# Encoder layer on one core: low parts of the first layer a step later, a norm in two steps, banks of attention's drain laid out anew

## The chip, the cores and the metric

The kernel runs on one core of a Trainium2 chip. The metric is the time of one execution on the device in microseconds (us); less is better. The core's engines work side by side, each through its own instructions in order: TensorE (PE in the profile, its weight loads PEld), VectorE (DVE), ScalarE (ACT), GpSimd (POOL), and SyncE (SP), which issues the DMAs. They wait for each other through semaphores. TensorE writes its results to PSUM, which has 8 banks; one bank holds 128 x 512 values of 32 bits.

## The reference

One encoder layer over 2048 tokens of width 1024, in 32-bit floating point. Cut to what matters here:

```
h = rms_norm(x);  z = h @ W_in
y_a = mlstm_group(...)                 # 4 heads, forward and backward
y_b = mla_group(...)                   # 4 heads, softmax over all keys
x = x + concat(y_a, y_b) @ w_out       # output projection, residual
h = rms_norm(x, g_ffn_norm)
x = x + square(relu(h @ w_ff1)) @ w_ff2   # 1024 -> 4096 -> 1024
```

## The kernel before

**Split products.** Every operand of a large matmul is split into a high part (a rounded copy, `fp32r`, made by ScalarE) and a low part (source less high part, a subtraction that VectorE makes, or POOL where `eng` says so): `split`, L44 to L52. `mm3` then issues three matmuls, high by high (L63), and two of a high and a low part (L64 and L65). In the trace a line of `split` is seen for all its callers, so one goes by the tiles' names.

**Stages.** The input projection takes the first 467 us, attention until some 1182 us, with the mLSTM's steps between its blocks; then come the output projection (`OutProj`), the feed-forward's first layer from 1372 us to about 2032 us, and the second layer.

**Attention.** A pair of a head and 256 queries is a block; there are 32. For each, `score` fills a bank `ps`, VectorE scales it into `p` and takes the maximum (L1016, L1020), ScalarE takes the exponential (L1027), `transpose_group` transposes into a bank `ptp` and splits that into `pth` and `ptl`, `pv` adds up in one bank `pv` for the block, and `out` scales that bank into `y` (L1063). `split_v` makes `vh` and `vl` of the values. There are 3 banks for `ps` and one for `pv`. While the last blocks drain, the weights of the output projection are split (`woh`, `wol`) and the first token tile is prepared: its mLSTM half is transposed into a bank (`pm`), split, and stored in ring buffers `r`.

**Output projection.** For each of 16 token tiles `prep_y` transposes into the bank `ypt` (pool `psY`) and splits into ring buffers; `project` issues the matmuls into two of the four banks of `psO` (`po`); `residual` adds the result to x (L1285). The last two tiles are projected together, with their residuals last. In the same time the operands of the first layer are prepared: tiles `h0` to `h6`, each of four pieces loaded into staging buffers `raw` and split into `h0h`, `h0l` and so on (`pieces_on`, `h_split`). The pools of PSUM take their banks in the order in which they are opened.

**First layer.** It is computed in blocks by the Strassen-Winograd scheme, with 7 products in place of 8. `layer1` runs over n = 0 to 31 (16 column blocks of W1 for each of two halves of the tokens); each n has 7 products of 12 matmuls into a bank `pu` (6 banks, `psF`), the evacuations (`evacuate`, L1500 and ScalarE's relu and square L1503, L1504), and combinations of results (`u_combine`, L1537). The order of the work is written by hand as generators that are advanced between the products: `wsteps` (`weights1`) makes the high and low parts of W1 in ring buffers `r`, some products ahead (`ahead`), and the sums of W1's blocks (`sw`, and in place in `w1raw`, L1377); `extra` is, one after the other, the remaining pieces of the first half's operands, `tokens` (norm, transposes `dpt`, combinations and stores of the second half's tokens) and `exchange` (the second half's operands are loaded into the low tiles and split in place while the first half's products finish, in n = 14 to 16, L1434 and L1435). The norm (`normalise`) sums squares on ScalarE, takes the root on POOL (`nr`, L59) and scales on VectorE (L1309).

Of the kernel before, what the change touches and what calls it, by code (L numbers as in the profile page):

```python
# [8 lines left out]
F32 = mybir.dt.float32  # L9
# [4 lines left out]
ALU = mybir.AluOpType  # L14
AX = mybir.AxisListType
PSUM = bass.MemoryType.PSUM
DRAM = bass.MemoryType.DRAM

P = 128
# [20 lines left out]

class Ctx:
    pass


def split(nc, hi, lo, src, g=None, eng=None):

    if g is None:
        nc.scalar.copy(hi, src)  # L48
        (eng or nc.vector).tensor_tensor(lo, src, hi.bitcast(F32), op=ALU.subtract)  # L49
    else:  # L50
        nc.scalar.activation(hi, src, AF.Copy, scale=g)
        nc.vector.scalar_tensor_tensor(lo, src, g, hi.bitcast(F32), op0=ALU.mult, op1=ALU.subtract)  # L52
# [872 lines left out]
def attention(c, keep, drain, project):  # L925

    nc, tc = c.nc, c.tc
    with ExitStack() as st:
# [46 lines left out]
        def split_v(h, j):  # L975
            raw = vraw.pop((h, j))
            vh = vp.tile([P, 4, DV], F32R, name="vh")
            vl = vp.tile([P, 4, DV], F32R, name="vl")
            split(nc, vh, vl, raw, eng=nc.gpsimd)
            V[h, j] = vh, vl  # L980

        def load_q(h, j):
# [67 lines left out]
        def pv(b, j):  # L1050
            h = b // NB
            if j == 0:
                pvs[b] = psV.tile([P, 256], F32, name="pv")
            th, tl = pts.pop((b, j))
            vh, vl = V[h, j]
            for k in range(4):
                mm3(nc, pvs[b], vh[:, k, :], vl[:, k, :], th[:, k, :], tl[:, k, :],
                    j == 0 and k == 0, j == 3 and k == 3)
# [25 lines left out]
        N = NH * NB  # L1084
# [93 lines left out]
class OutProj:  # L1178
# [48 lines left out]
    def open(self, ent):  # L1227
        pool = self.c.tc.tile_pool
        self.sp = ent(pool(name="o_s", bufs=2, reuse_waits="tile"))
        self.psT = ent(pool(name="o_psT", bufs=2, space=PSUM, reuse_waits="tile"))  # L1230
        self.psY = ent(pool(name="o_psY", bufs=1, space=PSUM, reuse_waits="tile"))
        self.psO = ent(pool(name="o_ps", bufs=4, space=PSUM, reuse_waits="tile"))

    def load_y(self, s):
        c, nc = self.c, self.c.nc
# [52 lines left out]
    def normalise(self, s):  # L1288
        x1 = self.x.pop(s)
        xs = [self.c.e[:, j, :] for j in range(2)]  # L1290
        normalise(self.c, self.sp, [x1[:, 0:512], x1[:, 512:]], xs, xs)

    def transposed(self, s):
        q = s % 2
# [4 lines left out]
def normalise(c, sp, x, out, junk):  # L1299

    nc = c.nc
    ms = sp.tile([P, 2], F32, name="nms")
    r = sp.tile([P, 1], F32, name="nr")
    for j in range(2):
        nc.scalar.activation(junk[j], x[j], AF.Square, scale=D ** -0.5, accum_out=ms[:, j:j + 1])
    nc.gpsimd.tensor_tensor(ms[:, 0:1], ms[:, 0:1], ms[:, 1:2], op=ALU.add)
    rsqrt(c, r, ms[:, 0:1], 1)
    for j in range(2):
        nc.vector.tensor_scalar(out[j], x[j], r, None, op0=ALU.mult)  # L1309

# [26 lines left out]
class FeedForward:  # L1337
# [41 lines left out]
    def w1_split(self, n, op):  # L1379
        if n < self.NU - 3:  # L1380
            w = self.ring.tile([P, 2, 4, P], F32R)
        else:
            w = self.ring.pool.tile([P, 2, 4, P], F32R, name="r0")
        wh, wl = w[:, 0], w[:, 1]
        split(self.c.nc, wh, wl, self.w1_part(n, WOPS[op]))
        self.w1[n, op] = wh, wl

    def weights1(self):

        N = 2 * self.NU  # L1390
        self.nsplit = 0
        self.w1_combine(0, "S1")
        self.w1_combine(0, "S2")
        for n in range(N):
            for q in range(7):
                self.w1_split(n, q)
                self.nsplit += 1
                yield
                if q == 0:
                    self.w1_combine(n, "S3")  # L1400
                elif q == 2:
                    self.w1_combine(n, "S4")
                elif q == 5 and n + 1 < N:
                    self.w1_combine(n + 1, "S1")
                elif q == 6:
                    if n + 2 < N:
                        self.load_w1(n + 2)
                    if n + 1 < N:
                        self.w1_combine(n + 1, "S2")
                yield  # L1410

    def h_load(self, g, op, k):
        nc = self.c.nc
# [13 lines left out]
    def exchange(self):  # L1427


        c, nc = self.c, self.c.nc  # L1430
        todo = []

        def place(hi, lo):
            nc.scalar.copy(hi, lo.bitcast(F32))  # L1434
            nc.vector.tensor_tensor(lo, lo.bitcast(F32), hi.bitcast(F32), op=ALU.subtract)  # L1435

        def load(hi, lo, src):
            nc.sync.dma_start(lo.bitcast(F32), src)
            todo.append((hi, lo))

        first = [[self.stage.tile([P, 512], F32R, name="raw") for _ in range(4)] for _ in range(2)]
        second = [[self.ring.pool.tile([P, 2, 512], F32R, name="r1") for _ in range(2)] for _ in range(2)]
        for k in range(4):
            load(first[0][k], first[1][k], c.d_h[1, 0, :, k, :])
            if k % 2:
                yield
        for k in range(2):
            load(second[0][k], second[1][k], c.d_h[1, 1, :, 2 * k:2 * k + 2, :])
        yield
        for _ in range(4):  # L1450
            place(*todo.pop(0))
            yield
        nxt = [first, [[t[:, k, :] for t in s for k in range(2)] for s in second]]
        for p in range(12):
            if p < 5:
                pool = self.hp if p < 3 else self.hp1
                hi, lo = (pool.tile([P, 4, 512], F32R, name=f"h{p}{part}") for part in "hl")
                nxt.append([[t[:, k, :] for k in range(4)] for t in (hi, lo)])
                for k in range(0, 4, 2):
                    load(hi[:, k:k + 2, :], lo[:, k:k + 2, :], c.d_h[1, p + 2, :, k:k + 2, :])  # L1460
            if p < 7:
                self.H[p] = nxt[p]
            place(*todo.pop(0))
            yield

    def h_pieces(self, g, todo):
# [78 lines left out]
    def tokens(self):  # L1545

        c, nc = self.c, self.c.nc
        for i in range(4):
            b = []
            for q in range(2):  # L1550
                t = 8 + 4 * q + i
                for j in range(2):
                    x = self.stage.tile([P, 512], F32, name="raw")
                    nc.sync.dma_start(x, c.d_x1[t * P:(t + 1) * P, j * 512:(j + 1) * 512])
                    b.append(x)
            junk = self.stage.tile([P, 512], F32, name="raw")
            for _ in range(4):
                yield
            for q in range(2):
                x = b[2 * q:2 * q + 2]  # L1560
                normalise(c, self.sp, x, x, [junk, junk])
                for _ in range(4):
                    yield
                transpose_x(c, self.psT, x, x)
                yield
            tt = [self.stage.tile([P, 512], F32, name="raw") for _ in range(3)]
            tt.append(junk)
            yield from combine_x(c, b, tt)
            store_x(c, 1, i, b, tt)
            for _ in range(4):  # L1570
                yield

    def layer1(self, extra):
        N = 2 * self.NU
        prev = None
        for n in range(N):
            g, f = divmod(n, self.NU)
            if n == 1:
                extra = self.tokens()
            elif n == self.NU - 2:  # L1580
                for _ in extra:
                    pass
                extra = self.exchange()
            for p in range(7):
                self.product(n, p)
                ahead = 7 * n + p + 1 + (5 if 0 < n < self.NU - 3 else 3)
                todo = min(2, ahead - self.nsplit)
                for i in range(todo):
                    next(self.wsteps, None)
                    if i + 1 < todo:  # L1590
                        next(self.wsteps, None)
                self.flush()
                if prev:
                    self.evacuate(*prev)
                prev = n, p, self.ps
                if todo > 0:
                    next(self.wsteps, None)
                if n > 0 and 1 <= p <= 4:
                    self.u_combine(n - 1, f"S{p}")
                next(extra, None)  # L1600
                if n == 0:
                    next(extra, None)
                if n == N - 1 and p == 2:
                    self.first2()
        return prev
# [145 lines left out]
def out_and_ffn(c):  # L1751
    tc = c.tc
    with ExitStack() as s_stage:
        with ExitStack() as s_e:
# [10 lines left out]
            with ExitStack() as s_y:  # L1765
# [45 lines left out]
                po = o.project(NT - 2, NT - 1)  # L1811
                s_wo.close()
                ff.open_h1(s_h1.enter_context)
                next(ff.wsteps)
                next(ff.wsteps)
                for _ in range(3):
                    pieces_on(4)
                for i in range(2):
# [53 lines left out]
```

## Time and profile before

| | us |
|---|---|
| median of 3 runs | 2649.92 (2648.83 to 2651.17) |
| the profiled execution | 2649.61 |
| its span | 2647.7 |
| TensorE busy | 2587.3 |
| VectorE busy | 1660.6 |
| ScalarE busy | 1201.9 |
| mean granted clock of TensorE | 0.995 |

The span runs from the first to the last instruction of the profiled execution; the execution's own time is 1.9 us longer. Busy is the time in which an engine had an instruction at work. The granted clock is the share of its full 2.4 GHz that TensorE was given; it knows two levels, 0.5 (1.2 GHz) and 1.

### The profile page before, as it was taken

To read this page: it belongs to the slowest core of one execution; us is meant where nothing else is said; L and a number is where in the kernel's file an instruction comes from. 1 tells how busy PE (TensorE), PEld (TensorE's weight loads), DVE (VectorE), ACT (ScalarE), POOL (GpSimd) and SP (SyncE) were. 2 spreads that over 40 slices of the span, in tenths; PEclk is the share of its full clock that TensorE was granted. 3 is DMA by queue.
4 is the path that set the end of the run, shared out by engine and by line. 5 is a ranking of instruction groups with operands and counts; after the bars stand their busy time and mean duration, and the time that the engine had idled before them with its cause. 6 is when DMAs were issued, how large, how long until landed. Compare 5 with 4: busy or idle time off the path is not lost. (4 is left out here: it accounts for less than half of the span.)

```text
span 2647.7 us, 37081 instructions
## 1 busy us (share of the span) xinstructions
PE 2587.3 (98%) x13227; PEld 2176.5 (82%) x13227; DVE 1660.6 (63%) x3202; ACT 1201.9 (45%) x2457; POOL 404.8 (15%) x442
## 2 busy tenths in 40 slices
PE   8999999999999999989999999999999999999999
PEld 6888888778888888878888877678887888888887
DVE  5585476655666666654367777777676477676443
ACT  6455443546666666651144444554544333332332
POOL 1211120123224232220000000000000133332000
PEclk9999999999999999999999999999999999999999
DMA  4345244355455464445665555834445744444552
GB/s 152 119 131 162 90 134 137 71 120 131 93 101 123 92 115 98 70 134 176 201 232 169 167 174 166 274 131 164 142 149 203 280 146 148 146 145 143 207 179 99
DMA packets 298293, 391.57 MB, mean 148 GB/s; under 512 B 33217, under 2 KB 187132, under 8 KB 298108
## 3 DMA queue, kind: packets, MB, share of 16 engines
q1 hardware_dynamic: 295804, 385.01, 49.1%
q10 hardware_dynamic: 2304, 4.20, 0.4%
q8 instruction: 104, 1.70, 0.3%
q14 instruction: 81, 0.66, 0.1%
HBM read 256.94 MB, written 132.17 MB: 147 GB/s over the span
## 5 line engine op out<-in xcount | busy, mean ns | idle before, releaser
L63 PE MATMUL pd<-w2h,uh 128*128 128x512 f32 x896 | 348.9, 389 | 1.3 <-ACT w2h L48 0.9
L64 PE MATMUL pd<-w2l,uh 128*128 128x512 f32 x896 | 348.8, 389 | 0.4 <-DVE w2l L49 0.4
L65 PE MATMUL pd<-w2h,ul 128*128 128x512 f32 x896 | 348.7, 389 | 0.0
L49 DVE TENSOR_TENSOR ptl<-ptp,pth 128x512 fp32r<-128x512 f32 x256 | 176.5, 690 | 212.2 <-ACT pth L48 208.3
L49 DVE TENSOR_TENSOR ul<-ur,uh 128x1024 fp32r<-128x1024 f32 x110 | 144.3, 1312 | 247.9 <-ACT uh L48 247.6
L48 ACT CAST uh<-ur 128x1024 fp32r<-128x1024 f32 x110 | 115.5, 1050 | 395.4 <-PE pd L64 382.4
L48 ACT CAST pth<-ptp 128x512 fp32r<-128x512 f32 x256 | 148.9, 584 | 239.0 <-PE ptp L1046 232.3
L1503 ACT ACTIVATE e<-e 128x512 f32<-128x512 f32 x128 | 80.9, 632 | 278.5 <-DVE e L1500 278.5
L63 PEld LDWEIGHTS pd<-w2h,uh 128*128 128x128 f32 x896 | 168.3, 188 | 36.8 <-ACT w2h L48 1.4
L1016 DVE TENSOR_SCALAR_CACHE_REDUCE p<-ps 128x512 f32<-128x512 f32 x256 | 175.0, 684 | 36.1 <-PE ps L1015 35.5
L64 PEld LDWEIGHTS pd<-w2l,uh 128*128 128x128 f32 x896 | 168.3, 188 | 35.5 <-DVE w2l L49 0.7
L65 PEld LDWEIGHTS pd<-w2h,ul 128*128 128x128 f32 x896 | 168.3, 188 | 34.8
L1646 POOL TENSOR_TENSOR r<-wr,r 128x512 f32<-128x512 f32 x48 | 88.5, 1843 | 634.2 <-DMA wr<-in_w 605.9
L49 DVE TENSOR_TENSOR r<-w1raw,r 128x512 fp32r<-128x512 f32 x160 | 110.5, 690 | 103.7 <-ACT r L48 102.5
L1046 PE MATMUL ptp<-ident,p 128*128 128x128 f32 x1024 | 154.3, 274 | 1.3 <-ACT p L1027 0.9
L63 PE MATMUL pz<-wh,hh 128*128 128x512 f32 (+1 forms) x384 | 150.7, 394 | 3.3 <-ACT hh L48 3.3
L1500 DVE TENSOR_TENSOR e<-pu,e 128x512 f32<-128x512 f32 x224 | 150.7, 685 | 3.2 <-PE pu L65 3.2
L65 PE MATMUL pz<-wh,hl 128*128 128x512 f32 (+1 forms) x384 | 151.0, 393 | 0.0
L64 PE MATMUL pz<-wl,hh 128*128 128x512 f32 (+1 forms) x384 | 150.8, 393 | 0.0
L63 PE MATMUL pv<-pth,vh 128*128 128x256 f32 x512 | 145.8, 285 | 4.3 <-DVE y L1063 2.5
L64 PE MATMUL pv<-ptl,vh 128*128 128x256 f32 x512 | 145.8, 285 | 1.2 <-DVE ptl L49 1.0
L65 PE MATMUL pv<-pth,vl 128*128 128x256 f32 x512 | 145.3, 284 | 0.0
(395 smaller groups left out, 6584.1 us busy)
## 6 DMA issues: line engine op xcount, KB each, us to landing
d_u<-e SPq DMA_DIRECT2D x224, 256.0 KB
ur<-d_u SPq DMA_DIRECT2D x110, 512.0 KB
w1raw<-in_w SPq DMA_DIRECT2D x64, 512.0 KB
wr<-in_w SPq DMA_DIRECT2D x96, 256.0 KB
raw<-in_w_in SPq DMA_DIRECT2D x48, 256.0 KB
xt<-in_x SPq DMA_DIRECT2D x16, 512.0 KB
mb<-d_M SPq DMA_DIRECT2D x32, 256.0 KB
r<-in_x SPq DMA_DIRECT2D x16, 512.0 KB
```

Source lines behind the costliest of these rows:

```text
L48: nc.scalar.copy(hi, src)
L49: (eng or nc.vector).tensor_tensor(lo, src, hi.bitcast(F32), op=ALU.subtract)
L63: nc.tensor.matmul(out, ah, bh, start=first, stop=False)
L64: nc.tensor.matmul(out, ah, bl, start=False, stop=False)
L65: nc.tensor.matmul(out, al, bh, start=False, stop=last)
L1016: nc.vector.tensor_scalar(probs[b, a][:, j, :], o, SCALE, None, op0=ALU.mult, op1=ALU.max, accum_out=maxes[b, a][:, j:j + 1])
L1046: nc.tensor.transpose(pt[:, k, :], p[:, j, k * P:(k + 1) * P], c.ident)
L1500: nc.vector.tensor_tensor(out, o, t, op=ALU.add)
L1503: nc.scalar.activation(t, t, AF.Relu)
L1646: nc.gpsimd.tensor_tensor(R, wr, R, op=ALU.subtract)
```

## The change

It has six edits. `split_v` makes the low parts of head 0's values on VectorE where POOL made them. `pv` of the last block takes a bank of the scores' pool. `OutProj.open` opens its three pools of banks in another order: `psO` first. `normalise` becomes a generator with a step between POOL's root and VectorE's scaling. `weights1` and `exchange` issue the low part one step behind its high part (`low`, a new helper), and `weights1` makes its combinations at other steps. And the number of steps that are run ahead of the products is changed, with two more steps between the last projection and the last pieces.

```diff
+def low(nc, hi, lo, src):
+    nc.vector.tensor_tensor(lo, src, hi.bitcast(F32), op=ALU.subtract)
...
-            split(nc, vh, vl, raw, eng=nc.gpsimd)
+            split(nc, vh, vl, raw, eng=nc.gpsimd if h else None)
...
-                pvs[b] = psV.tile([P, 256], F32, name="pv")
+                if b < N - 1:
+                    pvs[b] = psV.tile([P, 256], F32, name="pv")
+                else:
+                    pvs[b] = psS.tile([P, 512], F32, name="ps")[:, 0:256]
...
+        self.psO = ent(pool(name="o_ps", bufs=4, space=PSUM, reuse_waits="tile"))
+        self.psY = ent(pool(name="o_psY", bufs=1, space=PSUM, reuse_waits="tile"))
         self.psT = ent(pool(name="o_psT", bufs=2, space=PSUM, reuse_waits="tile"))
-        self.psY = ent(pool(name="o_psY", bufs=1, space=PSUM, reuse_waits="tile"))
-        self.psO = ent(pool(name="o_ps", bufs=4, space=PSUM, reuse_waits="tile"))
...
     rsqrt(c, r, ms[:, 0:1], 1)
+    yield
     for j in range(2):
         nc.vector.tensor_scalar(out[j], x[j], r, None, op0=ALU.mult)
...
-        split(self.c.nc, wh, wl, self.w1_part(n, WOPS[op]))
+        src = self.w1_part(n, WOPS[op])
+        self.c.nc.scalar.copy(wh, src)
         self.w1[n, op] = wh, wl
+        return lambda: low(self.c.nc, wh, wl, src)
...
+        last = None
+        for s in range(7 * N + 1):
+            if last:
+                last()
                 self.nsplit += 1
...
+            last = self.w1_split(*divmod(s, 7)) if s < 7 * N else None
+            yield
+            n, q = divmod(s - 1, 7)
+            if s and q == 0:
+                self.w1_combine(n, "S3")
+            elif s and q == 2:
+                self.w1_combine(n, "S4")
+            elif q == 4 and n + 1 < N:
+                self.w1_combine(n + 1, "S1")
+            elif q == 5 and n + 1 < N:
+                self.w1_combine(n + 1, "S2")
+            elif s and q == 6 and n + 2 < N:
+                self.load_w1(n + 2)
+            yield
...
+        half = []
+
+        def place():
+            if half:
+                low(nc, *half.pop())
+            if todo:
+                hi, lo = todo.pop(0)
+                nc.scalar.copy(hi, lo.bitcast(F32))
+                half.append((hi, lo, lo.bitcast(F32)))
...
-        for p in range(12):
+        for p in range(13):
...
-                normalise(c, self.sp, x, x, [junk, junk])
-                for _ in range(4):
+                yield from normalise(c, self.sp, x, x, [junk, junk])
+                for _ in range(3):
                     yield
...
-                ahead = 7 * n + p + 1 + (5 if 0 < n < self.NU - 3 else 3)
+                ahead = 7 * n + p + 1 + (3 if n == 0 else 5 if n < self.NU - 4 else 2)
...
-                next(ff.wsteps)
-                next(ff.wsteps)
+                for _ in range(4):
+                    next(ff.wsteps)
```

ScalarE at the first layer's entry, between the last projection and the first products, before (`r<-w1raw` and `r<-sw` are high parts of W1, `h3h` to `h6h` those of the tokens' operands):

```order
L48 CAST h2h<-raw 128x512 x4
L48 CAST r_14841<-w1raw_14747 128x512
L48 CAST r_14949<-sw 128x512
L48 CAST h3h<-raw 128x512 x4
L48 CAST h4h<-raw 128x512 x4
L48 CAST h5h<-raw 128x512 x4
L48 CAST r_15017<-w1raw_14749 128x512
L48 CAST r_15034<-w1raw_14747 128x512
L48 CAST h6h<-raw 128x512 x2
```

and of the change:

```order
L52 CAST h2h<-raw 128x512 x4
L1395 CAST r_14841<-w1raw_14747 128x512
L1395 CAST r_14948<-sw 128x512
L1395 CAST r_14952<-w1raw_14749 128x512
L52 CAST h3h<-raw 128x512 x4
L52 CAST h4h<-raw 128x512 x4
L52 CAST h5h<-raw 128x512 x4
L1395 CAST r_15020<-w1raw_14747 128x512
L1395 CAST r_15037<-sw 128x512
L52 CAST h6h<-raw 128x512 x2
```

A third high part of W1 now stands ahead of `h3h`, `h4h` and `h5h`, where it stood behind them.

VectorE at attention's start, from the end of the first row of scores to the scan L584 (L588 of the change), before:

```order
L1020 TENSOR_REDUCE nm<-mx 128x1
L571 TENSOR_SCALAR w<-e 128x128
L1016 TENSOR_SCALAR p,mx<-ps 128x512
L575 TENSOR_SCALAR d<-w 128x128
L576 TENSOR_TENSOR d<-e,d 128x128
L577 RECIPROCAL wi<-w 128x128
L578 TENSOR_TENSOR d<-d,wi 128x128
L1016 TENSOR_SCALAR p,mx<-ps 128x512 x2
L581 TENSOR_TENSOR ln<-ln,d 128x128
L582 SCALAR_TENSOR_TENSOR f<-f,ln 128x128
L584 SCALAR_TENSOR_TENSOR b<-f 128x128
```

and of the change:

```order
L1024 TENSOR_REDUCE nm<-mx 128x1
L53 TENSOR_TENSOR vl<-raw,vh 128x512
L575 TENSOR_SCALAR w<-e 128x128
L1020 TENSOR_SCALAR p,mx<-ps 128x512
L53 TENSOR_TENSOR vl<-raw,vh 128x512
L579 TENSOR_SCALAR d<-w 128x128
L580 TENSOR_TENSOR d<-e,d 128x128
L581 RECIPROCAL wi<-w 128x128
L582 TENSOR_TENSOR d<-d,wi 128x128
L1020 TENSOR_SCALAR p,mx<-ps 128x512
L53 TENSOR_TENSOR vl<-raw,vh 128x512
L1020 TENSOR_SCALAR p,mx<-ps 128x512
```

Three of the four subtractions `vl` that POOL made stand here between VectorE's other work; the fourth follows.

VectorE around a token norm of the first layer (`raw<-raw,nr` is the scaling, `e<-pu,e` an evacuation, `r<-w1raw,r` and `r<-sw,r` low parts of W1), before:

```order
L49 TENSOR_TENSOR r_16333<-sw,r_16333 128x512
L1500 TENSOR_TENSOR e<-pu,e 128x512
L1309 TENSOR_SCALAR raw<-raw,nr 128x512 x2
L49 TENSOR_TENSOR r_16362<-w1raw_16063,r_16362 128x512
L1500 TENSOR_TENSOR e<-pu,e 128x512
L1377 TENSOR_TENSOR sw<-w1raw_16222,w1raw_16224 128x512
L49 TENSOR_TENSOR r_16383<-w1raw_16063,r_16383 128x512
L1377 TENSOR_TENSOR sw<-sw,w1raw_16222 128x512
```

and of the change:

```order
L1519 TENSOR_TENSOR e<-pu,e 128x512
L1386 TENSOR_TENSOR sw<-w1raw_16225,w1raw_16227 128x512
L46 TENSOR_TENSOR r_16336<-w1raw_16066,r_16336 128x512
L1519 TENSOR_TENSOR e<-pu,e 128x512
L1386 TENSOR_TENSOR sw<-sw,w1raw_16225 128x512
L1318 TENSOR_SCALAR raw<-raw,nr 128x512 x2
L46 TENSOR_TENSOR r_16364<-w1raw_16066,r_16364 128x512
L1556 TENSOR_TENSOR e<-e 128x512
L46 TENSOR_TENSOR r_16387<-w1raw_16225,r_16387 128x512
```

The scaling stood right behind an evacuation and ahead of the low part of the same step; now two sums of W1, a low part and another evacuation of the step between stand ahead of it.

## Rows read from the trace of the kernel before

**Rows 1.** The page of the kernel before: span, engines, one group of operations.

```profile
span 2647.7 us, 37081 instructions
...
PE 2587.3 (98%) x13227; PEld 2176.5 (82%) x13227; DVE 1660.6 (63%) x3202; ACT 1201.9 (45%) x2457; POOL 404.8 (15%) x442
...
L49 DVE TENSOR_TENSOR r<-w1raw,r 128x512 fp32r<-128x512 f32 x160 | 110.5, 690 | 103.7 <-ACT r L48 102.5
```

**Rows 2.** Waits of TensorE, 1480 to 1830 us: total, times, longest.

```profile
PE dpt L1318 <- DVE raw L1309: 8.4, 3, 3.7
PE pu L63 <- ACT r L48: 4.6, 7, 0.8
PE pu L65 <- DVE r L49: 3.5, 6, 0.6
```

**Rows 3.** Busy us by stretch: PE, PEld, DVE, ACT, POOL; then granted clock, DMA.

```profile
1640.00:1740.00 100.00, 87.15 (x346) 63.36 (x345) 78.50 (x118) 51.16 (x82) 0.00 (x0) 0.98 0.67 224
1830.00:2032.00 202.00, 201.06 (x875) 164.02 (x873) 141.32 (x225) 98.60 (x168) 0.00 (x0) 1.00 0.45 153
1150.00:1200.00 50.00, 42.63 (x241) 36.13 (x241) 26.16 (x52) 26.34 (x55) 13.83 (x13) 0.93 0.53 142
```

**Rows 4.** Timeline at attention's start: start, duration, instruction [idle before, releaser].

```profile
474.43 1.13 ACT L48 CAST vh<-raw 128x512 fp32r<-128x512 f32 x2
...
475.11 5.20 POOL L49 TENSOR_TENSOR vl<-raw,vh 128x512 fp32r<-128x512 f32 x4 [5.34 <-ACT vh L48]
...
472.23 0.16 DVE L1020 TENSOR_REDUCE nm<-mx 128x1 f32<-128x4 f32 x1
...
477.21 0.60 DVE L581 TENSOR_TENSOR ln<-ln,d 128x128 f32<-128x128 f32 x1 [1.01 <-ACT ln L574]
477.84 1.34 DVE L582 SCALAR_TENSOR_TENSOR f<-f,ln 128x128 f32<-128x128 f32 x1
479.22 1.37 DVE L584 TENSOR_TENSOR_SCAN b<-f 128x128 f32<-128x128 f32 x1
...
481.60 0.42 DVE L587 TENSOR_TENSOR_SCAN cu<-u 128x128 f32<-128x128 f32 x1
...
481.23 0.50 PE L1011 MATMUL ps<-kh,qh 128*128 128x512 f32 x1 [2.47 <-DVE p L1016]
```

**Rows 5.** Timeline of attention's drain, VectorE and TensorE.

```profile
1165.97 0.69 DVE L49 TENSOR_TENSOR ptl<-ptp,pth 128x512 fp32r<-128x512 f32 x1 [1.52 <-ACT pth L48]
...
1181.18 0.68 DVE L49 TENSOR_TENSOR r<-pm,r 128x512 fp32r<-128x512 f32 x1
1181.99 0.42 DVE L1063 TENSOR_TENSOR y<-pv,rb 128x256 f32<-128x256 f32 x1
...
1167.80 0.36 PE L63 MATMUL pv<-pth,vh 128*128 128x256 f32 x1 [2.05 <-DVE y L1063]
...
1182.47 0.90 PE L1257 MATMUL ypt<-ident,r 128*128 128x128 f32 x4 [1.89 <-DVE y L1063]
```

**Rows 6.** Timeline of the first layer's entry, three engines.

```profile
1361.17 2.18 ACT L48 CAST h3h<-raw 128x512 fp32r<-128x512 f32 x4
...
1362.59 2.49 DVE L49 TENSOR_TENSOR h3l<-raw,h3h 128x512 fp32r<-128x512 f32 x4
...
1372.40 2.48 DVE L1285 TENSOR_TENSOR r<-po,r 128x512 f32<-128x512 f32 x4
...
1368.15 0.39 PE L65 MATMUL po<-woh,r 128*128 128x512 f32 x1
...
1372.45 0.40 PE L63 MATMUL pu<-h0h,r 128*128 128x512 f32 x1
```

**Rows 7.** Timeline of the longest token wait.

```profile
1545.27 0.88 DVE L1309 TENSOR_SCALAR raw<-raw,nr 128x512 f32<-128x512 f32 x2 [3.96 <-POOL nr L59]
...
1545.90 1.94 PE L1318 MATMUL dpt<-ident,raw 128*128 128x128 f32 x8 [3.67 <-DVE raw L1309]
```

**Rows 8.** The stretch behind that wait, columns as in the third group.

```profile
1545.90:1551.50 5.60, 5.60 (x18) 4.76 (x19) 4.33 (x8) 3.39 (x6) 0.00 (x0) 0.51 0.15 34
```

More of the change, by code (lines that the diff above doesn't have):

```diff
@@ L1290, in normalise @@
         xs = [self.c.e[:, j, :] for j in range(2)]
-        normalise(self.c, self.sp, [x1[:, 0:512], x1[:, 512:]], xs, xs)
+        for _ in normalise(self.c, self.sp, [x1[:, 0:512], x1[:, 512:]], xs, xs):
+            pass
     def transposed(self, s):
@@ L1393, in weights1 @@
         self.w1_combine(0, "S2")
-        for n in range(N):
-            for q in range(7):
-                self.w1_split(n, q)
+        last = None
+        for s in range(7 * N + 1):
+            if last:
+                last()
                 self.nsplit += 1
[L1398 to L1410, printed above, removed]
+            last = self.w1_split(*divmod(s, 7)) if s < 7 * N else None
[12 more added lines that the diff above has]
+            yield
     def h_load(self, g, op, k):
@@ L1431, in exchange @@
         todo = []
-        def place(hi, lo):
-            nc.scalar.copy(hi, lo.bitcast(F32))
-            nc.vector.tensor_tensor(lo, lo.bitcast(F32), hi.bitcast(F32), op=ALU.subtract)
+        half = []
[6 more added lines that the diff above has]
+                half.append((hi, lo, lo.bitcast(F32)))
         def load(hi, lo, src):
@@ L1450, in exchange @@
         for _ in range(4):
-            place(*todo.pop(0))
+            place()
             yield
         nxt = [first, [[t[:, k, :] for t in s for k in range(2)] for s in second]]
-        for p in range(12):
+        for p in range(13):
             if p < 5:
@@ L1462, in exchange @@
                 self.H[p] = nxt[p]
-            place(*todo.pop(0))
+            place()
             yield
```

## The prediction

> **What bounds the kernel.** I read the page first. TensorE is busy for 2587.3 us of a span of 2647.7 us [rows 1], so some 60 us are idle time and whatever is lost at a lower clock; the matmuls themselves stay as they are, and only this rest can be won or lost. Next I read the table of who waited for whom on TensorE, and then the same table by stage, to see which idle stretches lie where the change works. Of the waits, 8.4 us are three waits of the token transposes (`dpt`) for VectorE's scaling at L1309, and the two largest groups with matmuls of the first layer (`pu`), which wait for the high and low parts of W1, add up to 4.6 + 3.5 us [rows 2]. Those lie while the second half's operands are brought in: from 1640 to 1740 us TensorE works 87.15 of 100 us, so that 12.85 are idle, with VectorE at 78.50 [rows 3]. From 1830 us to the layer's end TensorE is busy for 201.06 of 202 us with VectorE at 141.32: there the layer has no waits left to take. The last step was the timeline of four places: attention's start [rows 4] and its drain [rows 5], the entry of the first layer [rows 6] and the worst token wait [rows 7]. The profiled execution took 2649.61 us, 0.3 us under the median of the three runs, so I make the sum against 2649.6 and read it as the median's too.
>
> **Attention's start: four low parts from POOL to VectorE.** On VectorE one 128x512 subtraction has a mean of 690 ns [rows 1], so four cost 2.4 to 2.8 us there. They also add a wait: the first now stands right behind the row maximum (`nm`, done at 472.39 us), and its high part, the first of two in 1.13 us, was only begun by ScalarE at 474.43 us, so VectorE, with the scores' scaling `p` queued behind it, stands still for some 2.6 us [rows 4]. Given back is what VectorE loses while POOL runs the four (5.20 us from 475.11 us): the scan at L584 took 1.37 us then and the like one at L587 0.42 us later, and L582 took 1.34 us; if that one too would need some 0.4, 1.9 us come back. So does VectorE's wait of 1.01 us for `ln` [rows 4]. 2.4 + 2.6 - 1.9 - 1.0 = 2.1 us is how much later the `p` comes for which TensorE waits 2.47 us there already [rows 4]; some of it will be caught up in the next waits, so I take **+1.3** (0 to +3). The Trainium skill (SBUF — State Buffer, "SBUF: two separate sides") says that a VectorE operation with two SBUF inputs and a GpSimd operation exclude each other for a whole instruction. By that rule more than my 1.9 us would come back and the term would be about 0; the scan's row agrees that something like it happens, but not how far.
>
> **Attention's drain: last values in a score bank.** `pv` of block 31 no longer needs the bank that `y` of block 30 frees; TensorE waited 2.05 us for it [rows 5]. It does not gain all of that, because its second matmul needs `ptl`, which ended at 1165.97 + 0.69 = 1166.66 us: some 1.3 us are won. At the end the transposes `ypt` waited 1.89 us for `y` (1181.99 + 0.42 us). With the banks laid out anew they wait for the low part of `pm` instead, begun at 1181.18 and done at 1181.86 us: 0.55 us less [rows 5]. The 50 us around them had a granted clock of 0.93 [rows 3], a loss of 3.5 us; with shorter waits I give back 1.6 us of it. That makes **-3.5**, with bounds of -1.5 (the clock stays low) and -5 (both dips gone).
>
> **Entry of the first layer: a new wait.** This term goes against the change. The two further `next(ff.wsteps)` put a third high part of W1 on ScalarE ahead of the splits of `h3`, `h4` and `h5`. Its ring buffer held the low part of the last but one token tile, which TensorE read until the matmul at 1368.15 us. Before, `h3h` began at 1361.17 and `h3l` at 1362.59 us; now ScalarE can go on only at 1368.5, does the W1 part in 0.6 us, and `h3l` starts near 1369.7, 7.1 us later. Behind it stand eight more low parts, the loads that need the staging buffers which these free, and the residual sums (begun at 1372.40 us before) [rows 6]. The banks make this matter: the projection now sits in banks 0 to 3, so that the first product needs the bank of the residual's first half, where banks 0 to 2 were free before. With all of the chain's idle time squeezed out, twelve casts of 0.54 us, a low part and a half of the residual end at 1369.1 + 6.5 + 0.7 + 1.2 = 1377.5 us; with none, 7.1 us after 1373.6, at 1380.7. The first product began at 1372.45 us [rows 6], so the stall is 5.1 to 8.2 us; I take 7.0, since the loads wait too. What follows such a wait is seen at 1545.90 us: after 3.67 us without work the next 5.6 us were granted 0.51, which costs 5.6 x 0.49 = 2.7 us [rows 7, 8]. So I take **+9.7** (+5 to +11). The Trainium skill (TensorE: Matmul & The Clock Gate, "HAM oscillation — how this bites in real kernels") has the rule that a wait of this kind lets the clock drop, so that the next burst starts cold. The row after the 3.67 us wait agrees; without the rule's effect the term would be 7.0 and the forecast 2.7 us lower.
>
> **Tokens: the norm in two steps.** The scaling at L1309 made VectorE stand still for 3.96 us until POOL's `nr` was there, and `dpt` then kept TensorE waiting 3.67 us [rows 7]. Now a step lies between the sums of squares and the scaling, and VectorE does other work in it. All three waits (8.4 us) should go, with the half clock behind the longest (2.7 us): **-11.1**. If the scaling, one step nearer to the transposes than before, still comes late, up to 4 us stay.
>
> **First layer and exchange: low parts one step later.** Before, VectorE stood idle for 102.5 us in all ahead of the low parts, waiting for ScalarE's high parts [rows 1], and so fell behind TensorE. Now high parts lie one step ahead. In the exchange VectorE is the limit, though: away from it it works 141.32 of 202 us [rows 3], that is 70% of a product of 12 x 201.06/875 = 2.76 us, or 1.93 us, and each of twelve steps adds a low part of 128x1024, as much as two of 128x512. Four of those one behind the other take 2.49 us [rows 6], so it costs 1.25 us; that is 3.18 us for a step, 12 x 0.42 = 5.0 us over TensorE's time. VectorE can run behind by a step or two before TensorE notices, but h4's two low parts come last and are needed at once, and so I leave 3.2 us (an estimate between 0 and the 5.0) of the 12.85: **-9.6** (-6 to -12.8). The number of steps that the weights run ahead, 2 from n = 12 on where it was 5 and then 3, I cost at nothing; VectorE's 30% of idle time hides it. If that cover fails, it is the rival below.
>
> **Sum.** 1.3 - 3.5 + 9.7 - 11.1 - 9.6 = -13.2, and 2649.6 - 13.2 = **2636.4 us**.
>
> **The rivals.** *The entry's wait does not cost anything* (the high part's buffer is free earlier than I think, or the first product gets a free bank): 2636.4 - 9.7 = 2626.7. For it: no wait stands at the entry now. Against: the named reader at 1368.15 us is in the trace. *The first layer's waits go by half only*, because VectorE's work and not its waits sets the pace: 10.4 us stay, 2646.8, within 0.2% of before (5.3 us, about what a measurement of this kernel can tell from no change). For it: VectorE already works 78.50 of 100 us in the exchange [rows 3], and 4.6 us of the waits were put down to ScalarE [rows 2]. *The other side:* with only 2 steps ahead from n = 12 on, the low part of each product comes late by a little at 20 x 7 = 140 products. From 13.2/140 = 0.09 us each it eats the gain; at 0.2 us the time is 2636.4 + 28 = 2664. Against: the 202 us with one busy TensorE and VectorE at 70% [rows 3], in which TensorE was idle for 0.9 us. *It doesn't do what it says:* TensorE's waits were for ScalarE's queue, which is as long as before; then the first layer gives nothing and start, drain and entry leave +7.5: 2657.
>
> **How the numbers follow.** My forecast gets 0.50, the entry without cost 0.20, half the gain 0.18, late low parts 0.06, no effect 0.06. The forecast's own range is 2630 to 2643 (the bounds of entry and exchange, taken together by halves); down to 2624 it takes in the second case, up to 2647 the third, and the two slower ones are left out. Faster by over 0.2%: 0.50 + 0.20 + a part of the third, 0.80; within 0.2%: 0.12; slower: 0.08.
>
> **What the profile after would show.** Right: no wait of `dpt` for its scaling; under 6 us of waits of `pu` near 1650 to 1740 us; a wait of 5 to 8 us of the first `pu` matmul for the residual sum, with a low clock behind it; `pv` and `ypt` waits in the drain under 1.5 us in all. Wrong: no wait at the entry (then the time is near 2627), waits of `pu` for the low parts spread from n = 12 to the end, or token waits that merely changed their releaser.

## Result and profile after

The changed kernel takes 2625.23 us (median of 4 runs, 2623.05 to 2626.28) against 2649.93 of the kernel before on the same chip: a ratio of 0.9906, with a 95% interval of 0.9888 to 0.9923. Forecast were 2636.4, with a range of 2624 to 2647: the way and the range held, but the time lies 1.2 us above the range's lower end, and the gain of 24.7 us is 1.9 times the 13.2 of the sum.

The page of the changed kernel, its span and the engines' busy time:

```profile
span 2624.4 us, 37119 instructions
...
PE 2578.9 (98%) x13227; PEld 2175.3 (83%) x13227; DVE 1659.3 (63%) x3206; ACT 1213.1 (46%) x2457; POOL 392.5 (15%) x438
```

The waits of TensorE (total, times, longest), the rows that answer to [rows 2, 5]:

```profile
PE pu L67 <- DVE r L1292: 8.0, 1, 8.0
...
PE pu L68 <- DVE h4l L46: 2.2, 2, 1.9
...
PE pv L67 <- ACT pth L52: 1.3, 1, 1.3
PE ypt L1264 <- DVE r L53: 1.3, 1, 1.3
```

The reader is to see two things. The waits of `dpt` and those for W1's parts, which led the list before, are gone; of the exchange 2.2 us for `h4l` are left. And the largest wait now is a new one: 8.0 us of the first layer's first matmul for the residual. One sign of the forecast did not come: the waits of `pv` and `ypt` in the drain were to be under 1.5 us in all, and they are 1.3 + 1.3 = 2.6.

TensorE issues the same matmuls in the same order in both kernels, so the start of one matmul can be set against the start of the same one in the other trace. Stages bounded in this way (in us, from the start of one matmul to that of another; the bounds lie at 467, 600, 1160, 1190, 1400, 1541.5, 1640 and 1750 us of the trace before):

| stage | before | before, second profile | changed |
|---|---|---|---|
| attention's start | 133.6 | 130.3 | 130.6 |
| attention | 559.9 | 560.0 | 561.0 |
| attention's drain | 29.5 | 29.7 | 26.2 |
| projection, entry | 210.1 | 210.2 | 220.8 |
| before the tokens' waits | 141.4 | 142.0 | 141.1 |
| tokens | 98.6 | 98.6 | 87.1 |
| exchange | 110.0 | 112.4 | 93.4 |

The second column is a further profile of the kernel before (below). Behind 1750 us the kernels take equally long (892.3 us to the last matmul). This table, and not the sum of idle time, shows where the time went: 3.3 us less in the drain, 10.6 more at the entry, 11.5 less at the tokens, 16.6 less in the exchange. The 3.0 us at attention's start are not the change's: the second profile of before lacks them too.

**The entry, as forecast.** The timeline of the changed kernel, ScalarE, VectorE and TensorE, which answers to [rows 6]:

```profile
1363.59 0.62 ACT L1395 CAST r<-w1raw 128x512 fp32r<-128x512 f32 x1 [8.04 <-PE po L69]
1364.12 2.18 ACT L52 CAST h3h<-raw 128x512 fp32r<-128x512 f32 x4
...
1373.53 0.62 ACT L52 CAST h5h<-raw 128x512 fp32r<-128x512 f32 x1 [2.35 <-DMA raw<-d_h]
...
1364.76 2.50 DVE L53 TENSOR_TENSOR h3l<-raw,h3h 128x512 fp32r<-128x512 f32 x4 [7.80 <-ACT h3h L52]
...
1374.79 2.48 DVE L1292 TENSOR_TENSOR r<-po,r 128x512 f32<-128x512 f32 x4
...
1375.62 0.77 PE L67 MATMUL pu<-h0h,r 128*128 128x512 f32 x1 [7.99 <-DVE r L1292]
```

ScalarE stands still for 8.04 us at the third high part of W1 until TensorE has read the buffer; `h3h` follows at 1364.12 us and `h3l` at once. The last piece of `h5` waits for its load, which waits for a staging buffer, the residual stands behind that, and the first product behind the residual. The clock of the two stretches behind it (columns as in [rows 3]):

```profile
1375.62:1380.88 5.26, 5.26 (x13) 4.10 (x14) 5.23 (x9) 1.12 (x3) 0.00 (x0) 0.50 0.62 218
1380.88:1386.14 5.26, 5.26 (x24) 4.26 (x23) 4.50 (x8) 2.66 (x5) 0.00 (x0) 1.00 0.25 85
```

Granted were 0.50 for 5.26 us and then 1.00; 13 matmuls are recorded in the first stretch and 24 in the second. The Trainium skill's rule that a wait of this kind ends in a cold start (TensorE: Matmul & The Clock Gate, "HAM oscillation — how this bites in real kernels") agrees with these rows.

**VectorE no longer waits for ScalarE's high parts.** Groups of instructions on VectorE (count, busy, mean ns, idle before and its releaser); the first answers to the last row of [rows 1]:

```profile
L46 DVE TENSOR_TENSOR r<-w1raw,r 128x512 fp32r<-128x512 f32 x160 | 109.4, 684 | 3.3 <-ACT r L1395 3.3
...
L46 DVE TENSOR_TENSOR r<-sw,r 128x512 fp32r<-128x512 f32 x64 | 43.8, 685 | 11.6 <-ACT r L1395 11.5
```

Waiting for ScalarE, it stood idle for 102.5 us ahead of the first group before and stands for 3.3 us now; ahead of the second, 41.5 us have become 11.5.

### The profile page after: what moved, and what is told of

It reads as the page before. It is cut to its first block, busy times and chain, and to the rows that moved or that the text cites. A ratio compares the mean times of both kernels' runs of the same rounds, so it can differ in the third digit from the quotient of the medians.

```text
span 2624.4 us, 37119 instructions
## 1 busy us (share of the span) xinstructions
PE 2578.9 (98%) x13227; PEld 2175.3 (83%) x13227; DVE 1659.3 (63%) x3206; ACT 1213.1 (46%) x2457; POOL 392.5 (15%) x438
## 5 line engine op out<-in xcount | busy, mean ns | idle before, releaser
L53 DVE TENSOR_TENSOR ul<-ur,uh 128x1024 fp32r<-128x1024 f32 x110 | 151.5, 1378 | 251.8 <-ACT uh L52 251.7
L1665 POOL TENSOR_TENSOR r<-wr,r 128x512 f32<-128x512 f32 x48 | 82.8, 1725 | 629.8 <-DMA wr<-in_w 614.6
L1395 ACT CAST r<-w1raw 128x512 fp32r<-128x512 f32 x160 | 98.3, 615 | 128.5 <-PE pu L69 114.7
L67 PE MATMUL pv<-pth,vh 128*128 128x256 f32 x496 | 140.4, 283 | 1.8 <-ACT pth L52 1.3
```

Of the source, the lines that this page charges most:

```text
L67: nc.tensor.matmul(out, ah, bh, start=first, stop=False)
L1395: self.c.nc.scalar.copy(wh, src)
L1665: nc.gpsimd.tensor_tensor(R, wr, R, op=ALU.subtract)
```

## The experiments

Six versions undo or move one part of the changed kernel each (e1 to e6), one makes one part alone (e9), and two put together what these showed (e7, e8). The bank of the last `pv` was not undone by itself. One table for all of them, with stages as above and the ratio of times to the kernel before, whose runs shared a chip with each:

| version | ratio to before | drain | projection, entry | tokens | exchange |
|---|---|---|---|---|---|
| before | 1 | 29.5 | 210.1 | 98.6 | 110.0 |
| the change | 0.9906 | 26.2 | 220.8 | 87.1 | 93.4 |
| W1 steps moved (e1) | 0.9878 | 25.3 | 212.2 | 87.0 | 93.3 |
| old banks (e2) | 0.9898 | 24.4 | 220.2 | 87.1 | 91.7 |
| values on POOL (e3) | 0.9906 | 25.3 | 220.3 | 87.0 | 91.7 |
| norm in one step (e5) | 0.9907 | 25.3 | 219.6 | 87.0 | 91.7 |
| old placing (e4) | 0.9931 | 25.3 | 220.1 | 87.0 | 100.2 |
| W1's low parts as before (e6) | 0.9940 | 26.7 | 211.0 | 90.2 | 107.0 |
| W1's low parts alone (e9) | 0.9906 | 27.6 | 210.6 | 87.1 | 100.2 |
| entry mended (e7) | 0.9864 | 26.4 | 210.1 | 87.1 | 91.7 |
| and exchange earlier (e8) | 0.9855 | 26.2 | 210.2 | 87.0 | 89.0 |

The intervals of the ratios are about 0.0015 to either side (0.0022 for e9).

**e1, W1's steps behind the pieces.**

```diff
-                for _ in range(4):
+                for _ in range(2):
                     next(ff.wsteps)
                 for _ in range(3):
                     pieces_on(4)
+                for _ in range(2):
+                    next(ff.wsteps)
```

> The changed kernel, with the two further steps of W1 behind the pieces of the operands and ahead of the residual. Theory (the high part of W1 on ScalarE holds up h3 to h5, and so the residual): the operands are split on time, the first product waits only for the residual behind the last of them, some 1.2 us, and the clock does not fall; the 10.0 us lost at the entry shrink to about 1.2, time 2616.5 (2614 to 2619). Rival (the new banks alone make the first product wait for the residual): the wait stays near 8 us and the time near 2625.

Measured: 2615.79 us, ratio 0.9878 [0.9864, 0.9893]; the entry's stage shrank by 8.5 us, as the theory had it. The wait of the first product in this run:

```profile
PE pu L67 <- DVE r L1292: 1.8, 1, 1.8
```

The high part on ScalarE is what made the residual late. The 1.8 us left I put to the bank; no run has the old banks with the steps moved in this way.

**e2, the projection's pools in the old order.**

```diff
-        self.psO = ent(pool(name="o_ps", bufs=4, space=PSUM, reuse_waits="tile"))
-        self.psY = ent(pool(name="o_psY", bufs=1, space=PSUM, reuse_waits="tile"))
         self.psT = ent(pool(name="o_psT", bufs=2, space=PSUM, reuse_waits="tile"))
+        self.psY = ent(pool(name="o_psY", bufs=1, space=PSUM, reuse_waits="tile"))
+        self.psO = ent(pool(name="o_ps", bufs=4, space=PSUM, reuse_waits="tile"))
```

> The changed kernel with the projection's pools opened in the old order. Theory (the late residual matters only because the first product needs its bank): no wait of the first product, since three free banks cover 8.2 us and the residual comes some 8 us late; the drain loses the shorter wait of ypt, 1 to 2 us; time 2616.7 (2615 to 2620). Rival (what is late is the operands themselves): waits of pu for h3l or h4l of some 5 us appear instead, time 2622 to 2626.

Measured: 2621.30 us, ratio 0.9898 [0.9883, 0.9912]; neither number came. The first product went without a wait, the second did not. The timeline, the residual on VectorE and the second product's first matmul:

```profile
1373.09 2.48 DVE L1292 TENSOR_TENSOR r<-po,r 128x512 f32<-128x512 f32 x4
...
1375.11 0.76 PE L67 MATMUL pu<-h1h,r 128*128 128x512 f32 x1 [7.17 <-ACT r L1395]
```

The matmul starts 0.2 us behind the third of the four residual operations (1373.09 + 3 x 0.6, an estimate from the row), as the first product of the changed kernel starts 0.2 us behind the first of them (1374.79 + 0.6). The trace names a cast that ends in the same 0.1 us; but the matmul waits for VectorE too, so I take the residual as the cause. Which bank ties the two the trace does not tell. So the old order covers one product, not three as I had thought, and the entry is hardly shorter for it: 220.2 against 220.8 us. The drain took 24.4 us here, no more than with the new order, and `ypt` does not wait at all: the new banks bring nothing there.

**e3, the values' low parts on POOL again.**

```diff
-            split(nc, vh, vl, raw, eng=nc.gpsimd if h else None)
+            split(nc, vh, vl, raw, eng=nc.gpsimd)
```

> The changed kernel with the low parts of head 0's values on POOL again. If the move costs 1.3 us, as forecast, the time falls to 2623.9. If it costs 0.7 us where it stands and the 3.1 us won near 564 us have another cause, the time is 2624.5 and no wait for kw stands at 564 us. If the gain near 564 us comes from the move, a wait of about 2 us returns there and the time is 2627.6.

Measured: 2623.72 us, ratio 0.9906 [0.9891, 0.9921], the changed kernel's own ratio. The stage of attention's start hardly tells the two apart either: it is 130.0 us here, 130.6 in the changed kernel and in e7, which has POOL too. Over all profiles but the first of before, it takes 129.6 to 130.6 us with POOL (five) and 130.6 to 131.4 with VectorE (six). The timeline of the changed kernel, VectorE and TensorE:

```profile
475.36 0.69 DVE L53 TENSOR_TENSOR vl<-raw,vh 128x512 fp32r<-128x512 f32 x1 [2.67 <-ACT vh L52]
...
482.04 0.43 DVE L588 TENSOR_TENSOR_SCAN b<-f 128x128 f32<-128x128 f32 x1
...
476.85 0.50 PE L1015 MATMUL ps<-kh,qh 128*128 128x512 f32 x1 [1.67 <-DVE p L1020]
...
479.71 0.73 PE L1015 MATMUL ps<-kh,qh 128*128 128x512 f32 x1 [1.45 <-DVE p L1020]
```

VectorE stands still for 2.67 us, as worked out, and TensorE waits for `p` 1.67 and 1.45 us, where it waited 2.47 us before [rows 4]. In e3 it waits 2.5 us for `p` and 0.6 for a transpose that does not wait in the changed kernel, so from 465 to 500 us its waits add up to 3.8 us in both. The scan of 128x128 (482.04 us) takes 0.43 us, with POOL idle. The same scan in e3, with POOL at work:

```profile
479.11 1.37 DVE L588 TENSOR_TENSOR_SCAN b<-f 128x128 f32<-128x128 f32 x1
```

Here it takes 1.37 us again. The Trainium skill (SBUF — State Buffer, "SBUF: two separate sides") has a VectorE operation with two SBUF inputs and a GpSimd operation that reads SBUF exclude each other for a whole instruction; these two rows agree that this scan is slowed while POOL works, and do not show how.

**e5, the norm in one step.**

```diff
-                yield from normalise(c, self.sp, x, x, [junk, junk])
-                for _ in range(3):
+                for _ in normalise(c, self.sp, x, x, [junk, junk]):
+                    pass
+                for _ in range(4):
                     yield
```

> The changed kernel with the norm of the tokens in one step again (the transposes keep their place). Theory (VectorE stands still at the scaling, some 4 us for each of eight norms, and the transposes behind it come late): waits of dpt return; all of it would be 11.6 us, but VectorE now enters them less late, so about 6 us, time 2631 (2628 to 2637). Rival (with the low parts a step later VectorE has room enough): no wait, 2625.

Measured: 2622.45 us, ratio 0.9907 [0.9891, 0.9924]. The rival was right: the tokens' stage takes 87.0 us as with the norm in two steps, and no wait of `dpt` is in the trace. My theory of the token waits fell with this run, and not because the standing still had gone. VectorE's scaling in the kernel before, and here (count, busy, mean ns, idle before and its releaser):

```profile
L1309 DVE TENSOR_SCALAR raw<-raw,nr 128x512 f32<-128x512 f32 x16 | 7.1, 484 | 19.0 <-POOL nr L59 19.0
...
L1318 DVE TENSOR_SCALAR raw<-raw,nr 128x512 f32<-128x512 f32 x16 | 7.0, 481 | 17.9 <-POOL nr L63 17.9
```

It still waits 17.9 us for the root where it waited 19.0, and none of that reaches TensorE.

**e4, the exchange's low parts right behind their high parts** (`place` and its calls as before, 12 steps).

```diff
+        def place(hi, lo):
+            nc.scalar.copy(hi, lo.bitcast(F32))
+            nc.vector.tensor_tensor(lo, lo.bitcast(F32), hi.bitcast(F32), op=ALU.subtract)
```

> The changed kernel with the exchange's low parts right behind their high parts again. Theory (in the exchange VectorE's waits for ScalarE's 1024 wide casts make it late, and with it the parts of W1): of the 16.6 us won there about half are lost again, with waits of pu for the low parts of h3 and h4 and for the parts of W1; time 2633 (2630 to 2638). Rival (only the parts of W1 matter): at most 3 us, 2625 to 2628.

Measured: 2630.67 us, ratio 0.9931 [0.9916, 0.9945]; the exchange took 100.2 us, 6.8 more than with the change: about what the theory said, and more than the rival's 3. Its waits between 1500 and 1760 us:

```profile
PE pu L69 <- DVE r L46: 6.3, 4, 1.7
PE pu L68 <- DVE h4l L1448: 1.7, 2, 0.9
PE pu L67 <- ACT h4h L1447: 0.3, 1, 0.3
```

**e6, W1's low parts right behind their high parts** (`weights1`, `w1_split` and `ahead` as before, two early steps).

```diff
-        src = self.w1_part(n, WOPS[op])
-        self.c.nc.scalar.copy(wh, src)
+        split(self.c.nc, wh, wl, self.w1_part(n, WOPS[op]))
         self.w1[n, op] = wh, wl
-        return lambda: low(self.c.nc, wh, wl, src)
```

> The changed kernel with W1's low parts right behind their high parts again, with the old steps ahead and the two early steps left out. At the entry this behaves as with the steps behind the pieces: about 8.8 us less. Theory (VectorE's standing still at each low part of W1 makes it late in tokens and exchange): some 8 to 12 us come back there, so the time is near 2625 (2623 to 2629), with waits of pu for W1's parts between 1640 and 1740 us. Rival (the exchange's own parts were the cause): no such waits, 2616 to 2618.

Measured: 2632.55 us, ratio 0.9940 [0.9923, 0.9956]. The entry went back to 211.0 us, but tokens took 3.1 us and the exchange 13.6 us more than with the change: 16.7 us where I expected 8 to 12, and so the time is above the 2623 to 2629 of the theory. VectorE's idle time ahead of the first group of W1's low parts is 116.7 us. Some 3.5 us of the exchange's 13.6 are the clock, an estimate from 50 us that were granted 0.90 at the end of the stage, 0.97 in the changed kernel. Some of TensorE's waits there:

```profile
PE pu L67 <- ACT r L52: 4.1, 6, 0.8
PE pu L68 <- DVE h3l L46: 3.0, 2, 1.9
PE dpt L1327 <- DVE raw L1318: 2.7, 2, 2.0
```

**e9, one part alone.** The kernel before with W1's low parts one step behind (the new `w1_split`, `weights1` and `ahead`, and this):

```diff
-                for _ in range(3):
+                for _ in range(5):
                     next(ff.wsteps)
```

> The kernel before with one part of the change alone: W1's low parts one step behind their high parts, with the new steps ahead; the two early steps stand behind the residual, ahead of the first product. Norm, exchange, drain, banks and attention's start are as before. If W1's low parts carry the gain, as the run without them says, the token waits go without the norm in two steps (11 us) and in the exchange some 10 us of the 16.6: time 2627 to 2629, ratio 0.992. If each part has its own share (norm: the token waits; exchange's placing: its waits), at most 8 us, ratio 0.997.

Measured: 2622.62 us (2622.02 to 2628.74), ratio 0.9906 [0.9884, 0.9928]: one part gives what the whole change gives, somewhat more than the 0.992 that I expected. It can, because it does not pay the changed kernel's 10 us at the entry (210.6 us here): its early steps stand behind the residual. Against e1, which hardly pays it either, it lacks 0.0028, some 7 us, and the exchange takes 7 us more. Tokens take 87.1 us, with the old norm: the time of the changed kernel. VectorE's first group shows the mechanism:

```profile
L46 DVE TENSOR_TENSOR r<-w1raw,r 128x512 fp32r<-128x512 f32 x160 | 109.4, 684 | 3.9 <-ACT r L1390 3.7
```

This part brings the new places of the combinations and the new number of steps ahead with it; no run takes these three apart. The exchange takes 100.2 us, as in e4, with the same waits:

```profile
PE pu L69 <- DVE r L46: 6.3, 4, 1.7
PE pu L68 <- DVE h4l L1443: 1.7, 2, 0.9
PE pu L67 <- ACT h4h L1442: 0.3, 1, 0.3
```

**A second profile of the kernel before (b0).** In its first profile the mLSTM's matmuls waited at 563.84 us:

```profile
563.84 0.66 PE L694 MATMUL pm<-v,kw 128*64 128x129 f32 x8 [2.15 <-issue]
```

> The kernel before once more, for one look. If the wait of 2.15 us of the mLSTM's matmuls near 564 us and the low clock behind it belong to the kernel, they stand there again; if they were one execution's DMA, they are gone, and then 3 us of the difference of the two profiled executions are not the change's.

The same instruction in the second profile, which ran 2649.61 us too:

```profile
561.88 0.66 PE L694 MATMUL pm<-v,kw 128*64 128x129 f32 x8 [0.36 <-issue]
```

The wait belongs to one execution. The second profile has a longer exchange in its place (112.4 us), with no more idle time there (12.56 us against 12.85) but a lower clock (granted 0.95 in the stage, 0.98 in the first profile): there are 2 to 3 us by which one execution's stages differ from another's.

**e7, the entry mended** (with the values on POOL).

```diff
-                for _ in range(4):
+                for _ in range(2):
                     next(ff.wsteps)
-                for _ in range(3):
+                for _ in range(2):
                     pieces_on(4)
                 for i in range(2):
                     o.residual(NT - 2 + i, po[i])
+                for _ in range(2):
+                    next(ff.wsteps)
+                pieces_on(4)
```

> The changed kernel with POOL making head 0's low parts, and at the entry two steps of W1, two groups of pieces, the residuals, two steps of W1, the last group of pieces. Theory: the residual no longer stands behind the operand that arrives last, so the first product waits for nothing; against the version with the steps alone moved (ratio 0.9878) the wait of 1.8 us and 0.9 us at attention's start go, ratio 0.9866, some 2614. Rival: h5 or W1's low part, now behind the residual, makes a later product wait as long; ratio 0.987 to 0.988.

Measured: 2611.95 us, ratio 0.9864 [0.9849, 0.9878]; the entry's stage takes 210.1 us, as in the kernel before. The one wait left in the first layer:

```profile
PE pu L68 <- DVE h4l L46: 2.2, 2, 1.9
```

**e8, the exchange a step earlier** (on e7).

```diff
+        place()
         for _ in range(4):
             place()
             yield
...
-        for p in range(13):
+        for p in range(12):
```

> The version with the entry mended, and the exchange's placing begun one part earlier (two high parts in its first step, so that every later low part comes one step sooner). Theory (the last wait in the exchange, 1.9 us for h4's second low part, and the half clock behind it are VectorE being late by less than a step): both go, 5 us less than with the entry alone, ratio 0.9847. Rival (the earlier casts now wait for their loads and hold up ScalarE): waits of pu near 1650 us instead, no gain.

Measured: 2608.39 us (2606.80 to 2612.77), ratio 0.9855 [0.9838, 0.9871]. No wait of TensorE between 1500 and 1760 us is left, and the exchange takes 89.0 us against 91.7. That is 2.7 us, not 5: in e7 the wait was not followed by a lowered clock, so little but itself was to be won. The intervals of e7 and e8 overlap; that e8 is faster is seen in the stage, not proved by the time. It is the fastest version measured. Its times come from another chip than the changed kernel's; by the two ratios it lies 0.0051 under that one, some 14 us, and its stages add up to 17 us less.

## Why the prediction was right and where it was wrong

**Entry: mechanism and size right.** Forecast +9.7, measured 10.6 (8.0 us of wait and a lowered clock). e1 and e7 show the high part on ScalarE and the residual's place as the cause. Wrong was the step "the banks make this matter": with the old order (e2) the wait moves to the second product, and the entry costs as much.

**Drain: size right, in part by luck** (-3.5 against -3.3). TensorE's idle time in the stage fell by 2.0 us, from 6.9 to 4.9, where 1.9 were forecast; but the banks have no share in it, as the old order (e2) is as short. By that the last `pv` in a score bank is what counts, which no run shows by itself. The rest is the clock, and it changes from one execution to the next: from 1155 to 1195 us the kernel before was granted 0.91, the changed one 0.96 and e1 1.00. But e9, which has the drain as before, was granted 0.96 too and took 27.6 us: at the same clock the edits are worth 27.6 - 26.2 = 1.4 us.

**Attention's start: too much.** Forecast +1.3; the ratio of e3 shows nothing, and the stages of single profiles differ by more than what is left, which is under 1 us. VectorE's standing still came as computed, and `p` came late by it; but a transpose's wait went in return, so that TensorE's waits there add up to 3.8 us with POOL (e3) and without.

**Tokens: size right, cause only half right.** Forecast -11.1, measured -11.5. I put all of it to the norm in two steps. Alone, that norm does most of it: e6, with the new norm and W1's low parts as before, takes 90.2 us where the kernel before takes 98.6, and has 2.7 us of waits left. But W1's low parts alone do all of it: e9, with the old norm, takes 87.1 us and has no wait, and e5, with the old norm in the changed kernel, likewise. So in the change as a whole the norm added nothing. The step that failed is "VectorE stands still at the scaling, and so the transposes are late": in e5 VectorE stands still for 17.9 us and the transposes are on time. That its wait of 3.96 us [rows 7] reached TensorE because VectorE was late already fits this, but is argued and not shown.

**Exchange: the term that was mis-sized.** Forecast -9.6, measured -16.6. I took 12.85 us of idle time as what could be won. But the idle column begins at the modelled end of a matmul, and more than the idle time is lost around a wait. The timeline of the kernel before:

```profile
1705.83 0.39 PE L65 MATMUL pu<-h6h,r 128*128 128x512 f32 x1
1707.05 0.50 PE L63 MATMUL pu<-raw,r 128*128 128x512 f32 x1 [0.83 <-ACT r L48]
1707.39 0.40 PE L64 MATMUL pu<-raw,r 128*128 128x512 f32 x1
1708.39 0.50 PE L65 MATMUL pu<-raw,r 128*128 128x512 f32 x1 [0.61 <-DVE r L49]
1708.73 0.40 PE L63 MATMUL pu<-raw,r 128*128 128x512 f32 x1
1708.96 0.40 PE L64 MATMUL pu<-raw,r 128*128 128x512 f32 x1
```

Matmuls that follow without a wait start 0.23 us apart (the last two). The waiting one came 0.83 + 0.39 = 1.22 us behind its predecessor, and the next came 0.34 us behind it. That is 1.56 us for two steps that take 0.46: a loss of 1.1 us for 0.83 of idle time. The stage has 20 waits before, and behind 18 of them the next matmul came 0.33 or 0.34 us later. 20 x 0.27 = 5.4 us, 110.0 x 0.02 = 2.2 us for the granted clock of 0.98, and the 12.85 idle make 20.4 (an estimate). By the version without waits (e8) the stage lost 110.0 - 89.0 = 21.0 us. Of that the change took 16.6 and left 4.4; the 3.2 that I left were of the right size, and the wait that is left is that for `h4l`, as forecast.

**The rivals.** That VectorE's work, and not its waits, sets the pace of the exchange is not borne out: its waits for ScalarE ahead of W1's low parts fell from 102.5 to 3.3 us in the first group, and the stage came within 4.4 us of the shortest, in which TensorE does not wait at all (e8). Two steps ahead from n = 12 on cost nothing: from 1750 us on the kernels take equally long. The time came out near the 2626.7 us of the rival without a wait at the entry, but not by it, and that is luck: the entry cost what was forecast, and the exchange gave more.

**What stays open.** The four stages make -3.3 + 10.6 - 11.5 - 16.6 = -20.8 us; with the other three of the table it is -23.0, where the two profiled executions differ by 23.4 and the medians by 24.7. Against the second profile of before the four are -3.5 + 10.6 - 11.5 - 19.0 = -23.4 us. The interval of the ratio, 0.0077 to 0.0112 of 2649.93 or 20 to 30 us, holds both; which execution is the typical one the two profiles cannot tell.

## What to carry to other kernels

Where one engine makes the first half of a result and another the second, put the second half a step later in program order: the waiting engine then has work, and here that one part gave as much as all six together, one of which cost 10 us at the entry. Before costing waits by their idle time, measure the stage between two instructions that both versions share: many short waits cost more than their idle time. And when work is put earlier on an in-order queue, look at who still reads its buffer: one cast ahead of its time cost 8 us.

## What was not expected of the hardware

A waiting matmul started 0.39 us and its idle time behind its predecessor, and the next one 0.34 us behind it, where 0.23 is usual for both steps, so that such a wait cost some 0.3 us over its idle time. VectorE's scan of 128x128 took 1.37 us while POOL subtracted, and 0.43 us without.

And a wait of TensorE of 1.9 us was followed by a lowered clock in some executions and not in others. The exchange's last wait in the changed kernel, and in e7:

```profile
1715.24 0.65 PE L68 MATMUL pu<-h4l,r 128*128 128x512 f32 x1 [1.88 <-DVE h4l L46]
1715.69 0.63 PE L69 MATMUL pu<-h4h,r 128*128 128x512 f32 x1
...
1703.20 0.50 PE L68 MATMUL pu<-h4l,r 128*128 128x512 f32 x1 [1.88 <-DVE h4l L46]
1703.54 0.39 PE L69 MATMUL pu<-h4h,r 128*128 128x512 f32 x1
```

Granted were 0.69 from 1717 to 1720 us in the first and 1.00 from 1703.5 to 1706.5 us in the second. With the same wait the stage took 93.3 us in e1, as in the first, and 91.7 in e2, e3 and e5, as in the second.
